# Five sets of down-projection weight sums moved behind the first product's loads, one of four subtractions on VectorE, the sums respread over the stages before

## The chip, the cores and the metric

The kernel runs on one core of one Trainium2 chip. Its time is the device time of one execution in microseconds (us); lower is better. Of the engines of a core, five matter here: TensorE (PE in the profile; PEld is its weight load), VectorE (DVE), ScalarE (ACT), GpSimd (POOL) and SyncE (SP), which in this kernel issues the DMAs.

## The reference

One layer of a decoder trunk for 1024 positions of width 1024, in float32: a token mixer (an RWKV-7 head group beside a causal convolution) and then a gated MLP with a short causal convolution. The change touches the MLP:

```python
def _conv_ffn(h, ffn_up, ffn_conv_w, ffn_conv_b, ffn_down):
    hid = h @ ffn_up.astype(h.dtype)
    hid = _causal_dwconv(hid, ffn_conv_w, ffn_conv_b)
    gate, up = hid[..., :D_FF], hid[..., D_FF:]
    return (jax.nn.gelu(gate, approximate=True) * up) @ ffn_down.astype(h.dtype)
```

Here D_FF is 2816: ffn_up is 1024 x 5632, ffn_down 2816 x 1024, and the convolution is 3 positions wide.

## The kernel before

**Products in three parts.** A float32 product is made from two halves of each operand. `split` (line 167) makes them: ScalarE casts the operand to the matmul type (the high part, `wh` or `w` for a weight, `a` for an activation), then an engine subtracts that from the operand (the low part, `wl`, or a second `w` or `a`). Three matmuls per tile follow: high by high, high by low, low by high (line 140). The subtraction for a weight runs on GpSimd, in `ffn_down` on VectorE (line 1140 sets that). `weight` loads a weight tile (line 175) and splits it; the last load issued is kept in `self.load`, the last low part in `self.low`.

**Seven products for eight.** The second half of the MLP's up-projection and the whole down-projection use sums of weight blocks and of activation blocks, so that seven block products give what eight would. A set of weight sums takes four 128x512 blocks b11, b12, b21, b22 and makes four results in place, with four operations on GpSimd (`four_sums`, line 1090).

**Who makes the sums.** For the up-projection, `act_sums` makes the activation sums `S` in twelve steps, and `shared` runs 16 blocks over them, each of 60 matmuls: five weights, 12 matmuls each. The first block loads its sums from DRAM; each of the other 15 loads four blocks of ffn_up (line 1056) into one of two groups of four buffers and calls `four_sums` itself, two blocks ahead of its use. For the down-projection, the generator `weight_sums` makes 12 sets (11 of ffn_down, and as third the one of the first shared block). Each set is four loads of 256 KB (line 1111), four GpSimd operations and four stores to DRAM (line 1114), from which products of `ffn_down` load their weights later. Its buffers hold two sets.

**The order of the stages.** The `gates` stage (a first pass over part of the up-projection); then six plain blocks (`PLAIN`, `ffn_pair`), each followed by `beside`, which takes one step of each generator handed to it and holds the step's instructions back behind a gate, a low part and a load of the block; then the 16 shared blocks; then `ffn_down` with seven products X, Y, ... of 11 steps j each (a step: split an activation, load and split a weight, 12 matmuls). The tile scheduler orders instructions on each engine by priority and expected readiness. `issue_after(x)` adds that an instruction is not placed ahead of x, on the same engine; SyncE's queue issues DMAs in order, and a DMA waits for the one eight earlier.

**Where the sets are made before.** Three sets in `gates`, one after each of the six plain blocks, and the last three in the first product, by `rest` on odd steps. There the call stands under high priority (`with first():`), and nothing holds its instructions: the scheduler put those three sets at the head of the shared stage, some 240 us ahead of the first product. In `shared` all four sums are GpSimd's.

Of the kernel before, what the change touches and what calls it, by code (L numbers as in the profile page):

```python
# [17 lines left out]
ALU = mybir.AluOpType  # L18
# [4 lines left out]
P = 128  # L23
# [79 lines left out]
class Trunk:  # L103
# [934 lines left out]
    def shared(self, i, S, A22, act0, act1, raws):  # L1038

        nc = self.nc  # L1040
        temp = lambda: self.f2p.tile([P, HALF], F32, tag="f2", name=self.nm("acc"))
        kview = lambda t: t.rearrange("p (k m) -> p k m", k=4)
        up = self.a["ffn_up"]

        def add(out, x, y):
            with self.tc.high_priority():
                nc.vector.tensor_tensor(out, x, y, ALU.add)

        if raws is None:
            T = lambda n: self.weight(kview(self.usums[n - 1]), [P, 4, P])  # L1050
            b22 = lambda: self.weight(up[FT + i, 1], [P, 4, P])
        else:
            with self.tc.high_priority():
                b11, b12, b21, b22r = raws
                for n in (1, 3, 0, 2):
                    self.load = nc.sync.dma_start(kview(raws[n]), up[n % 2 * FT + i, n // 2])
                t3 = self.wp.tile([P, HALF], F32, tag="wr", bufs=3, name=self.nm("t3"))
                self.four_sums(b11, b12, b21, b22r, t3)

            def pair(raw):  # L1060
                with self.tc.high_priority():
                    hi, lo = (self.wp.tile([P, HALF], F32R, tag=t, bufs=2, name=self.nm(t)) for t in ("wh", "wl"))
                    self.low = self.split(hi, lo, raw, True)[1]
                return kview(hi), kview(lo)

            T = lambda n: pair((b12, b11, t3, b21)[n - 1])
            b22 = lambda: pair(b22r)
        x, y, z = (self.bank() for _ in range(3))
        self.four(x, T(2), S[2], True, True)
        add(act1, act1, x)  # L1070
        self.four(y, T(1), S[1], True, True)
        W = temp()
        add(W, act1, y)
        self.four(z, T(3), S[3], True, True)
        add(x, W, z)
        self.four(y, b22(), S[4], False, True)
        add(y, act1, y)
        self.four(z, T(4), A22, False, True)
        add(z, act1, z)
        two = [temp() for _ in range(2)]  # L1080
        self.taps(0, i, 1, y, two[0])
        nc.vector.tensor_tensor(act0, act0, two[0], ALU.mult)
        self.taps(1, i, 0, z, act1)
        nc.scalar.activation(z, act1, AF.Gelu_apprx_tanh)
        self.taps(1, i, 1, x, two[1])
        nc.vector.tensor_tensor(act1, z, two[1], ALU.mult)

    def four_sums(self, b11, b12, b21, b22, t3):

        sub = lambda o, x, y, op=ALU.subtract: self.nc.gpsimd.tensor_tensor(o, x, y, op)  # L1090
        sub(t3, b22, b12)
        sub(b12, b12, b11)
        sub(b11, t3, b11, ALU.add)
        sub(b21, b21, b11)

# [41 lines left out]
    def ffn_down(self, acts, sums):  # L1137
        nc = self.nc
        first = self.tc.high_priority
        self.low_pool = False  # L1140
        A11, A12, A21, A22 = acts[0][:HT], acts[0][HT:], acts[1][:HT], acts[1][HT:]
        B = lambda r, c: lambda j: self.a["ffn_down"][c, ORDER[r * HT + j]]
        T = lambda n: lambda j: self.sums[n - 1, j]
        X = [self.bank() for _ in range(4)]
        Y = [self.bank(t) for t in ("pb", "pb", "pn", "pn2")]
        halves = lambda: [row[:, c * 512:(c + 1) * 512] for row in (self.row("nrow", 4) for _ in range(2)) for c in range(2)]
        four = lambda: [self.tp.tile([P, 512], F32, tag="tp", name=self.nm("c")) for _ in range(4)]

        def tt(out, a, b, op=ALU.add):
            nc.vector.tensor_tensor(out, a, b, op)  # L1150
            return out

        def s3(j):
            return tt(self.f2p.tile([P, HALF], F32, tag="f2", name=self.nm("s3")), A11[j], A21[j], ALU.subtract)

        def product(banks, src, wt, start, after, then=lambda j: None, held=(), soon=True):
            ops, n = [], HT - len(held)
            for j in range(HT):
                with first():
                    hi, lo = self.pair("a", self.h1p)  # L1160
                    self.split(hi, lo, src(j))
                    then(j)
                wh, wl = self.weight(wt(j), [P, 512], held=self.h1p if j % 2 else None) if j < n else held[j - n]
                op = (hi, wh), (hi, wl), (lo, wh)
                if j >= n:
                    ops.append(op)
                else:
                    for t in range(4):
                        mms(banks[t], t, op, start and j == 0, j == HT - 1)

            ins = []
            for t in range(4):
                for i, op in enumerate(ops):
                    ins += mms(banks[t], t, op, False, i == len(held) - 1)
                with first() if soon else ExitStack():
                    after(t)
            self.chain(ins)

        def mms(ps, t, op, start, stop):
            return [self.mm(ps, a[:, t * P:(t + 1) * P], w, start=start and i == 0, stop=stop and i == 2, skip=True)  # L1180
                    for i, (a, w) in enumerate(op)]

        def norm(h, t, c, f, src, junk):
            nc.scalar.activation(junk, src, AF.Square, accum_out=self.fss[:, 4 * h + t, c:c + 1])
            tt(f, src, self.post_ffn[:, c * 512:(c + 1) * 512], ALU.mult)

        def rest(j):
            if j % 2:
                next(sums, None)

        s1, s7 = halves(), halves()
        product(X, lambda j: A11[j], B(0, 0), True, lambda t: nc.scalar.copy(s1[t], X[t]), rest)
        list(sums)
        product(Y, s3, T(3), True, lambda t: nc.scalar.copy(s7[t], Y[t]))
        c11 = four()
        product(X, lambda j: A12[j], B(1, 0), False, lambda t: norm(
            0, t, 0, c11[t], X[t], self.f2p.tile([P, 512], F32, tag="f2", name=self.nm("junk"))))
        c21 = four()
        late = []

        def hold(j, every=2):

            if j % every == 1 and len(late) < HELD:
                home = self.hp if len(late) < HELD - 1 else self.ap
                late.append(self.weight(B(1, 1)(HT - HELD + len(late)), [P, 512], held=home))


        def after4(j):
            tt(A22[j], A21[j], A22[j])

        def after5(j):
            hold(j, 3)
            tt(A11[j], A22[j], A11[j], ALU.subtract)

        def after6(j):
            hold(j)
            tt(A12[j], A12[j], A11[j], ALU.subtract)

        product(Y, lambda j: A22[j], T(4), False, lambda t: tt(c21[t], s1[t], Y[t]), after4)
        product(X, lambda j: A22[j], T(1), True, lambda t: tt(s7[t], s7[t], X[t]), after5)  # L1220

        def second(t):
            tt(c21[t], c21[t], Y[t])
            tt(s1[t], s1[t], Y[t])
            norm(1, t, 0, c21[t], c21[t], Y[t])
            tt(s7[t], s7[t], s1[t])
            norm(1, t, 1, s7[t], s7[t], Y[t])
            self.ffn_out(4 + t, (c21[t], s7[t]), ready[4] if t == 3 else self.load_x1(4 + t, self.f2p, "f2"))

        def last(t):  # L1230
            tt(s1[t], s1[t], X[t])
            norm(0, t, 1, s1[t], s1[t], X[t])
            self.ffn_out(t, (c11[t], s1[t]), ready[t])

        with first():
            ready = [self.load_x1(t, self.ap, "act") for t in (0, 1, 2, 3, 7)]
        product(Y, lambda j: A11[j], T(2), True, second, after6, soon=False)
        product(X, lambda j: A12[j], B(1, 1), False, last, held=late)


    def run(self):
        nc = self.nc
# [5 lines left out]
        with ExitStack() as ctx:  # L1248
# [5 lines left out]
            sums = self.weight_sums()  # L1254
# [7 lines left out]
            ss = self.act_sums(h0, h1, S)  # L1262
            for i in range(PLAIN):
                nc.sync.dma_start(self.plain[i], self.ffn_pair(1, h1, i, temp))
                self.beside(sums, ss, ss)
            list(ss)
            raws = [self.h1p.tile([P, HALF], F32, tag="h", name=self.nm("b")) for _ in range(8)]

# [246 lines left out]
```

## Time and profile before

| what | value |
|---|---|
| median of 3 runs | 1285.8 us (1285.29 to 1287.09) |
| the profiled execution, its own time | 1284.83 us |
| its span, first to last instruction | 1283.1 us |
| mean granted TensorE clock | 0.984 |
| shared blocks 1 and 2 | 820 to 865 us |
| shared blocks 3 to 16 | 865 to 1063 us |
| products 1 and 2 of `ffn_down` | 1063 to 1123 us |
| products 3 to 7 | 1123 to 1283 us |

The profile shows one execution. A row of a group of instructions has line, engine, operation, output and inputs by name, count, busy time, mean duration, and idle time of the engine ahead of them with what ended it. A row of the waits has the engine and what it was about to do, what it waited for, the us in total, the number of waits and the longest. A row of a timeline has start and duration in us, the operation, how many in a row (x4), and in brackets the idle time ahead with what ended it. A row of the windows has the stretch, its length, the busy time of PE, PEld, DVE, ACT and POOL (with counts), the granted TensorE clock, the busy share of the DMA engines and their GB/s. The plain, shared and down-projection stages are read apart, since different engines wait in them.

### The profile page before, as it was taken

How to read it: one execution, taken by the hardware profiler on the slowest of the kernel's cores; microseconds unless marked ns; L12 is line 12 of the kernel's file. 1: busy time of each engine (PE TensorE's matmuls, PEld its weight loads, DVE VectorE, ACT ScalarE, POOL GpSimd, SP SyncE). 2: the span in 40 equal slices, each digit the busy share in tenths (PEclk: the TensorE clock that was granted, in tenths of full speed). 3: DMA queues.
4: the chain of work that ended last, by engine and by line, in shares of the span. 5: the costliest groups of instructions: out<-in, count | busy, mean ns of one | idle time of the engine just before them, and what ended most of it. 6: DMA issues, size and time to landing. Idle time of an engine off the chain costs nothing.

```text
span 1283.1 us, 22908 instructions
## 1 busy us (share of the span) xinstructions
PE 1215.2 (95%) x8388; PEld 979.9 (76%) x8388; DVE 912.6 (71%) x1570; ACT 728.2 (57%) x1516; POOL 517.9 (40%) x456
## 2 busy tenths in 40 slices
PE   6989999999999989999999999869999999999997
PEld 4767777787778867787798787657887878888885
DVE  5286998997679989995711756736765778569668
ACT  6563563655844865666742778625555555554451
POOL 4343320011113332344452698798888860000001
PEclk9999998999999999999999999989999999999999
DMA  7644442343343451233364998963222216346423
GB/s 237 174 134 137 118 130 75 98 133 126 107 132 87 127 193 57 93 91 111 112 173 128 335 343 295 349 201 106 76 74 74 82 54 218 99 130 206 126 81 131
DMA packets 104992, 184.64 MB, mean 144 GB/s; under 512 B 15184, under 2 KB 21712, under 8 KB 104880
## 3 DMA queue, kind: packets, MB, share of 16 engines
q1 hardware_dynamic: 104880, 183.18, 45.1%
q8 instruction: 66, 1.08, 0.3%
q14 instruction: 46, 0.38, 0.1%
HBM read 139.49 MB, written 43.65 MB: 143 GB/s over the span
## 4 chain that ended last, share of the span: by engine, by line
PE 45%; DVE 11%; DMA 6%; POOL 5%; issue 3%; ACT 3%; SPq 0%; POOLq 0%; DVEq 0%; ACTq 0%
PE pb L140 20%; PE pe L140 11%; PE xs L140 9%; POOL wl L167 3%; DVE pc L423 2%; PE Y L140 2%; POOL b L1090 2%; PE pc L140 2%; DMA b<-ffn_up 1%; DMA sums<-b 1%; DMA act<-early 1%; DVE nrow L1150 1%; DVE x L1134 1%; DMA pt<-mixd 1%; DMA x1d<-nrow 1%
## 5 line engine op out<-in xcount | busy, mean ns | idle before, releaser
L167 POOL TENSOR_TENSOR wl<-wr,wh 128x512 fp32r<-128x512 f32 (+1 forms) x145 | 188.9, 1304 | 219.9 <-ACT wh L167 190.9
L140 PE MATMUL pb<-h,wh 128*128 128x512 f32 (+3 forms) x720 | 229.6, 398 | 3.1 <-ACT wh L167 1.6
L140 PE MATMUL pb<-f,wh 128*128 128x512 f32 x592 | 188.0, 398 | 3.9 <-DVE pt L907 1.7
L167 ACT CAST wh<-wr 128x512 fp32r<-128x512 f32 (+1 forms) x184 | 113.0, 615 | 130.0 <-issue 36.3
L423 DVE SCALAR_TENSOR_TENSOR pc<-c,params,pc 128x512 f32<-128x512 f32 x232 | 174.2, 751 | 8.2 <-ACT pc L420 4.1
L140 PEld LDWEIGHTS pb<-h,wh 128*128 128x128 f32 (+2 forms) x720 | 131.9, 189 | 35.9 <-ACT wh L167 3.7
L140 PE MATMUL pb<-h,wl 128*128 128x512 f32 (+3 forms) x360 | 146.6, 407 | 2.1 <-POOL wl L167 2.0
L140 PEld LDWEIGHTS pb<-f,wh 128*128 128x128 f32 x592 | 109.9, 189 | 28.9 <-ACT wh L167 3.8
L140 PE MATMUL pb<-f,wl 128*128 128x512 f32 x296 | 117.7, 398 | 2.4 <-POOL wl L167 2.4
L1090 POOL TENSOR_TENSOR b<-b,b 128x512 f32<-128x512 f32 x78 | 104.2, 1341 | 7.0 <-DMA sums<-b 3.5
L162 POOL TENSOR_TENSOR ss<-var,mhalf 128x1 f32<-128x1 f32 x16 | 11.0, 693 | 223.2 <-DVE ss L1131 198.6
L167 POOL TENSOR_TENSOR wl<-b,wh 128x512 fp32r<-128x512 f32 x60 | 77.9, 1299 | 31.5 <-ACT wh L167 29.4
L140 PEld LDWEIGHTS pb<-h,wl 128*128 128x128 f32 (+2 forms) x360 | 67.7, 188 | 20.5 <-POOL wl L167 4.3
L167 ACT CAST wh<-b 128x512 fp32r<-128x512 f32 x60 | 37.0, 618 | 81.6 <-PE pb L140 34.4
L140 PE MATMUL pe<-f,wh 128*128 128x512 f32 x256 | 79.7, 393 | 0.1
L140 PEld LDWEIGHTS pb<-f,wl 128*128 128x128 f32 x296 | 55.8, 189 | 16.9 <-POOL wl L167 4.6
L167 DVE TENSOR_TENSOR a<-act,a 128x512 fp32r<-128x512 f32 x66 | 44.6, 693 | 22.9 <-ACT a L167 20.6
L167 ACT CAST a<-act 128x512 fp32r<-128x512 f32 x66 | 39.5, 618 | 37.3 <-PE Y L140 20.5
L140 PEld LDWEIGHTS pe<-f,wh 128*128 128x128 f32 x256 | 48.1, 189 | 10.1 <-ACT wh L167 0.5
L140 PE MATMUL xs<-f,wh 128*128 128x512 f32 x176 | 54.5, 391 | 0.4 <-DVE act L987 0.4
L713 POOL TENSOR_TENSOR XG<-r,GE 64x256 f32<-64x256 f32 x30 | 20.8, 694 | 84.3 <-DVE r L732 79.3
L140 PE MATMUL pe<-f,wl 128*128 128x512 f32 x128 | 50.8, 397 | 3.8 <-POOL wl L167 3.8
(431 smaller groups left out, 2986.8 us busy)
## 6 DMA issues: line engine op xcount, KB each, us to landing
wr<-ffn_up SPq DMA_DIRECT2D x81, 256.0 KB, 2.8
wr<-w_in SPq DMA_DIRECT2D x80, 256.0 KB, 2.9
b<-ffn_up SPq DMA_DIRECT2D x64, 256.0 KB, 2.6
b<-ffn_down SPq DMA_DIRECT2D x44, 256.0 KB, 4.5
sums<-b SPq DMA_DIRECT2D x44, 256.0 KB, 3.9
wr<-sums SPq DMA_DIRECT2D x44, 256.0 KB, 2.7
lows<-wl SPq DMA_DIRECT2D x40, 256.0 KB, 3.3
wl<-lows SPq DMA_DIRECT2D x40, 256.0 KB, 2.7
```

Of the source, the lines that this page charges most:

```text
L140: return self.nc.tensor.matmul(out, lhsT, rhs, start=start, stop=stop, skip_group_check=skip)
L162: self.nc.gpsimd.tensor_tensor(out, v[:, :n], self.mhalf[:, :n], ALU.pow)
L167: return self.nc.scalar.copy(hi, src), eng.tensor_tensor(lo, src, hi.bitcast(F32), ALU.subtract)
L423: nc.vector.scalar_tensor_tensor(out, c[:, j:j + HALF], w(j), acc, ALU.mult, ALU.add)
L713: nc.gpsimd.tensor_tensor(x[64:128], R[64:128, gs], w.GE[64:128, c, gs].unsqueeze(2).broadcast_to([64, 4, CH]), ALU.mult)
L1090: sub = lambda o, x, y, op=ALU.subtract: self.nc.gpsimd.tensor_tensor(o, x, y, op)
L1134: nc.vector.scalar_tensor_tensor(x, f[c], s[:, 1:2], x, ALU.mult, ALU.add)
L1150: nc.vector.tensor_tensor(out, a, b, op)
```

## The change

Three edits.

- `four_sums` takes an engine for its second operation, b12 - b11. `shared` hands it VectorE: 15 operations. The sets of `weight_sums` keep GpSimd for all four.
- After the plain blocks, a step of `weight_sums` is taken at blocks 0, 1, 3 and 4 only (four sets, not six). `act_sums` takes three steps at each of the first two blocks and two at the others (before: two at each), so that its twelve steps are done after the fifth block, not the sixth.
- In the first product, `rest` is called after the weight's load, on even steps j, not under high priority, and its instructions are held behind that step's weight load (`self.load`) and low part (`self.low`). Five sets are left for it. The call `list(sums)` behind the first product goes.

```diff
-                self.four_sums(b11, b12, b21, b22r, t3)
+                self.four_sums(b11, b12, b21, b22r, t3, nc.vector)
...
-    def four_sums(self, b11, b12, b21, b22, t3):
+    def four_sums(self, b11, b12, b21, b22, t3, eng=None):
...
-        sub(b12, b12, b11)
+        (eng or self.nc.gpsimd).tensor_tensor(b12, b12, b11, ALU.subtract)
...
                     self.split(hi, lo, src(j))
+                    if then is not rest:
+                        then(j)
+                wh, wl = self.weight(wt(j), [P, 512], held=self.h1p if j % 2 else None) if j < n else held[j - n]
+                if then is rest:
                     then(j)
-                wh, wl = self.weight(wt(j), [P, 512], held=self.h1p if j % 2 else None) if j < n else held[j - n]
...
         def rest(j):
-            if j % 2:
-                next(sums, None)
+            if j % 2 == 0:
+                with self.tc.issue_after(self.load.ins), self.tc.issue_after(self.low.ins):
+                    next(sums, None)
...
-        list(sums)
...
-                self.beside(sums, ss, ss)
+                self.beside(*[sums] * (i % 3 < 2), *[ss] * (3 if i < 2 else 2))
```

Line numbers in the changed kernel: the moved subtraction is line 1092, the other sums stay on 1090; lines behind the middle of the file are 3 higher.

Three places in the engines' queues show it. First GpSimd at the head of the shared stage. `wl_` are low parts, `t_` and `b_93..`/`b_92..` sums of shared blocks 2 and 3, `b_11...` sums of the sets. Before:

```order
L167 TENSOR_TENSOR wl_9420<-wr_9417,wh_9419 128x512
L1090 TENSOR_TENSOR b_9320<-b_9320,b_9319 128x512
L1090 TENSOR_TENSOR b_11309<-b_11309,b_11307 128x512
L1090 TENSOR_TENSOR b_9316<-b_9316,b_9315 128x512
L1090 TENSOR_TENSOR b_11370<-b_11370,b_11368 128x512
L1090 TENSOR_TENSOR b_9319<-t_1486_9467,b_9319 128x512
L1090 TENSOR_TENSOR b_9315<-t_1505_9592,b_9315 128x512
L1090 TENSOR_TENSOR b_11368<-b_11368,b_11367 128x512
L1090 TENSOR_TENSOR b_9321<-b_9321,b_9319 128x512
L167 TENSOR_TENSOR wl_9476<-b_9319,wh_9475 128x512
```

After, at the same place:

```order
L167 TENSOR_TENSOR wl_9369<-wr_9366,wh_9368 128x512
L1090 TENSOR_TENSOR t_1478_9435<-b_9290,b_9288 128x512
L1090 TENSOR_TENSOR t_1497_9560<-b_9286,b_9284 128x512
L167 TENSOR_TENSOR wl_9388<-wr_9385,wh_9387 128x512
L1090 TENSOR_TENSOR b_9287<-t_1478_9435,b_9287 128x512
L1090 TENSOR_TENSOR b_9283<-t_1497_9560,b_9283 128x512
L1090 TENSOR_TENSOR b_9289<-b_9289,b_9287 128x512
L1090 TENSOR_TENSOR b_9285<-b_9285,b_9283 128x512
L167 TENSOR_TENSOR wl_9444<-b_9287,wh_9443 128x512
```

The operations of the three sets and the b12 - b11 of blocks 2 and 3 are gone from between the low parts of the first block (`wl_9420`, now `wl_9388`, is its last) and the first low part of the second (`wl_9476`, now `wl_9444`). The moved b12 - b11 stand on VectorE, `L1092`, behind the taps and the first additions of the stage:

```order
L907 SCALAR_TENSOR_TENSOR acc_9273<-pb_9236,params,acc_9273 128x510
L920 TENSOR_TENSOR acc_9229<-pb_9192,acc_9273 128x512
L1047 TENSOR_TENSOR xs_99<-acc_9345,pe_9307 128x512
L1092 TENSOR_TENSOR b_9288<-b_9288,b_9287 128x512
L1092 TENSOR_TENSOR b_9284<-b_9284,b_9283 128x512
L1047 TENSOR_TENSOR xs_100<-act_9292,xs_100 128x512
L907 SCALAR_TENSOR_TENSOR acc_9404<-xs_100,params,acc_9404 128x511
```

On GpSimd, the sum that writes `b_9287` overwrites what this subtraction of `b_9288` reads, so it comes after it.

Second, SyncE's queue at the first product. `wr_` are weights of the steps j, `act_` activations fetched back, `b_` loads of a set, `sums<-` its stores. Before, weights follow each other, and step 5's is `wr_11443`:

```order
L1288 DMA act_11246<-early 128x512
L175 DMA wr_11405<-ffn_down 128x512
L1288 DMA act_11254<-plain 128x512
L1288 DMA act_11247<-early 128x512
L1288 DMA act_11255<-plain 128x512
L175 DMA wr_11443<-ffn_down 128x512
L175 DMA wr_11465<-ffn_down 128x512
L175 DMA wr_11487<-ffn_down 128x512
```

After, step 5's is `wr_11411`:

```order
L1291 DMA act_11214<-early 128x512
L175 DMA wr_11373<-ffn_down 128x512
L1291 DMA act_11222<-plain 128x512
L1291 DMA act_11215<-early 128x512
L1291 DMA act_11223<-plain 128x512
L1111 DMA b_11321<-ffn_down 128x512
L1111 DMA b_11322<-ffn_down 128x512
L1111 DMA b_11379<-ffn_down 128x512
L1111 DMA b_11380<-ffn_down 128x512
L1111 DMA b_11381<-ffn_down 128x512
L1111 DMA b_11382<-ffn_down 128x512
L175 DMA wr_11411<-ffn_down 128x512
```

Six loads of the second and third of the five sets stand ahead of it; two more (`b_11319`, `b_11320`) stand ahead of the activations.

Third, GpSimd behind the last low part of the shared stage. Before, the small operations of the output norm follow (`ss_`), near the end of the kernel:

```order
L167 TENSOR_TENSOR wl_11169<-t_1712_11125,wh_11168 128x512
L167 TENSOR_TENSOR wl_11186<-b_9322,wh_11185 128x512
L167 TENSOR_TENSOR wl_11203<-b_9321,wh_11202 128x512
L162 TENSOR_TENSOR ss_12933<-var_12935,mhalf 128x1
L162 TENSOR_TENSOR ss_12953<-var_12955,mhalf 128x1
```

After, 16 operations of four sets stand there; the first set of the five stands among the low parts of the two last shared blocks:

```order
L167 TENSOR_TENSOR wl_11154<-b_9290,wh_11153 128x512
L167 TENSOR_TENSOR wl_11171<-b_9289,wh_11170 128x512
L1090 TENSOR_TENSOR b_11322<-b_11322,b_11320 128x512
L1092 TENSOR_TENSOR b_11320<-b_11320,b_11319 128x512
L1090 TENSOR_TENSOR b_11319<-b_11322,b_11319 128x512
L1090 TENSOR_TENSOR b_11382<-b_11382,b_11380 128x512
L1090 TENSOR_TENSOR b_11321<-b_11321,b_11319 128x512
```

So the GpSimd work that stood at the head of the shared stage stands at the head of the down-projection.

## The prediction

> **What bounds the kernel now.** The page first: TensorE is busy for nearly the whole span, at a clock near full, and the chain that ended last is mostly its own.
>
> ```profile
> span 1283.1 us, 22908 instructions
> PE 1215.2 (95%) x8388; PEld 979.9 (76%) x8388; DVE 912.6 (71%) x1570; ACT 728.2 (57%) x1516; POOL 517.9 (40%) x456
> PE 45%; DVE 11%; DMA 6%; POOL 5%; issue 3%; ACT 3%; SPq 0%; POOLq 0%; DVEq 0%; ACTq 0%
> ```
>
> So time can be had only where TensorE waits or is slowed. The windows by stage show where (columns: stretch, length, busy time of PE, PEld, DVE, ACT, POOL, granted clock, DMA share, GB/s); the fourth row is an undisturbed pair of shared blocks.
>
> ```profile
> 760.00:820.00 60.00, 56.93 (x244) 44.89 (x243) 42.71 (x65) 46.70 (x97) 51.70 (x42) 1.00 0.90 320
> 820.00:865.00 45.00, 31.71 (x112) 22.92 (x111) 18.42 (x27) 15.67 (x33) 40.45 (x33) 0.85 0.74 259
> 865.00:1063.00 198.00, 196.70 (x852) 157.56 (x851) 132.97 (x190) 110.84 (x232) 160.34 (x122) 1.00 0.28 84
> 1007.46:1035.09 27.63, 27.63 (x121) 22.07 (x120) 18.03 (x27) 15.13 (x32) 23.69 (x19) 1.00 0.29 86
> 1063.00:1123.00 60.00, 59.91 (x264) 49.24 (x263) 41.66 (x66) 32.21 (x63) 0.00 (x0) 1.00 0.46 145
> ```
>
> Shared blocks 1 and 2 take 45.0 us; a later pair takes 27.6. The loss is 17.4 us, at a clock of 0.85, while GpSimd is busy 40.45 of 45. In the other 14 shared blocks TensorE is busy 196.70 of 198, in products 1 and 2 59.91 of 60, with GpSimd idle. TensorE's waits between 820 and 866 give the causes:
>
> ```profile
> PE pe L140 <- ACT wh L167: 4.7, 1, 4.7
> PE pe L140 <- POOL wl L167: 4.2, 3, 2.2
> PE xs L140 <- DVE s L167: 3.1, 1, 3.1
> PE pb L140 <- DVE pe L1047: 0.9, 1, 0.9
> PE pb L140 <- DVE acc L1047: 0.4, 1, 0.4
> ```
>
> They sum to 13.3 us; the other 4.1 of the 17.4 are matmuls at a lower clock behind the gaps. The ScalarE wait is GpSimd's in disguise: that cast takes a finished sum as input. GpSimd's timeline there:
>
> ```profile
> 828.85 1.28 POOL L1090 TENSOR_TENSOR b<-b,b 128x512 f32<-128x512 f32 x1 [3.46 <-DMA sums<-b]
> ...
> 838.77 5.45 POOL L1090 TENSOR_TENSOR b<-b,b 128x512 f32<-128x512 f32 x4
> 844.19 2.49 POOL L1090 TENSOR_TENSOR b<-t,b 128x512 f32<-128x512 f32 x2
> 846.63 2.50 POOL L1090 TENSOR_TENSOR b<-b,b 128x512 f32<-128x512 f32 x2
> 849.09 2.50 POOL L167 TENSOR_TENSOR wl<-b,wh 128x512 fp32r<-128x512 f32 x2
> 851.54 5.00 POOL L1090 TENSOR_TENSOR b<-b,b 128x512 f32<-128x512 f32 x4
> ```
>
> GpSimd works without a gap at 1.25 us an operation, and the second block's first low part comes at 849.09. It also sat 3.46 us behind a store of a set, whose buffer a held-up sum needed.
>
> **Edit 1: three sets leave the head of the shared stage.** In the changed order six sum operations of the three sets go from between 828.85 and 849.09 (7.5 us at 1.25), and two b12 - b11 go to VectorE (2.5 us); the 3.46 us wait on a store has no cause left. That is up to 13.5 us of earliness for the second block's first low part. What is late next is still GpSimd: within block 1's 13.8 us (half of 27.63) it has to run four low parts, six sums and one low part of block 2, 11 x 1.25 = 13.8 us, behind a cast that itself waits for a sum. I estimate 3.3 us of wait there, 1.7 in block 1 for the low parts, and half a us elsewhere: 5.5 us left of 17.4, a **gain of 12**. Bounds: 9.2 (7.5 for the sums ahead, 1.7 for the wait that one of them causes in block 1) and 17.4. I lie between because the new count of GpSimd operations just equals the time there is.
>
> The low clock goes with the gaps. Two windows of 4 us show it:
>
> ```profile
> 844.00:848.00 4.00, 1.85 (x4) 1.16 (x4) 2.09 (x3) 1.79 (x4) 4.00 (x5) 0.64 0.70 238
> 848.00:852.00 4.00, 1.82 (x5) 1.31 (x5) 0.00 (x0) 0.00 (x0) 4.00 (x4) 0.50 0.65 201
> ```
>
> Behind the 4.7 us gap the clock is 0.50. The Trainium skill (TensorE: Matmul & The Clock Gate, Part 1: The HAM clock gate) says that the clock halves only after an idle window of about 3.4 us; by that rule the 3.3 us I leave would cost no clock and the gain would be up to 1 us more. Since this trace is at 0.50 after one longer gap, it does not decide that.
>
> **Edit 2: b12 - b11 of 15 shared blocks on VectorE.** 15 operations leave GpSimd, but GpSimd is not late in the later blocks: it waits there for buffers that TensorE frees. Rows of the waits from 866 to 1048, of GpSimd and of VectorE:
>
> ```profile
> POOL wl L167 <- ACT wh L167: 25.7, 27, 2.6
> DVE acc L907 <- ACT fcarry L900: 15.7, 10, 1.6
> DVE pb L1047 <- PE pb L140: 16.9, 8, 3.2
> ```
>
> VectorE's share of it, 15 x 0.69 = 10.4 us, or 15 x 1.8 = 27 us with contention, lies in its 65 us of idle time (198 - 132.97), such as these waits. A new wait comes with it: GpSimd's third sum overwrites b11, which the moved subtraction reads, so GpSimd's queue, with the low parts behind it, waits for VectorE's queue, which itself waits up to 3.2 us for TensorE. GpSimd has 37.7 us idle in 14 blocks (198 - 160.34), 2.7 a block, and gains 1.25 a block: 3.9 against 3.2. I take **0**; the bounds are 0 and the 10.4 us of VectorE work should nothing cover it.
>
> **Edit 3: sums respread over the plain blocks.** Two sets fewer on GpSimd, the same `act_sums` work a block earlier on VectorE and ScalarE, which have 17 and 13 us idle of 60. The last `s` parts were the 3.1 us wait above; that is in edit 1's 17.4. TensorE idles 3.07 us in 760 to 820. I take **0**, bounds 3.1 gained, and, with one third more `act_sums` work in the first two blocks, as much lost.
>
> **Edit 4: five sets in products 1 and 2.** Two costs. First the loads. Product 1's loads already arrive just in time:
>
> ```profile
> 1064.00:1066.00 2.00, 2.00 (x11) 1.65 (x10) 2.00 (x5) 2.00 (x6) 0.00 (x0) 1.00 1.04 402
> 1067.17 11.44 SPq L175 DMA_DIRECT2D wr<-ffn_down x6
> 1072.50 0.62 ACT L167 CAST w<-wr 128x512 fp32r<-128x512 f32 x1 [4.16 <-DMA wr<-ffn_down]
> 1077.22 1.52 PE L140 MATMUL xs<-w,a 128*128 128x512 f32 x6
> ```
>
> The DMA engines run at 402 GB/s; step 5's weight arrives at 1072.5, and TensorE uses it at 1077.22, 4.7 us later. The change issues six or eight loads of 256 KB ahead of it, 1.6 or 2.1 MB at 402 GB/s, 3.9 or 5.2 us. With a cast (0.62) and a subtraction on VectorE (0.68 to 1.8) behind it, the weight is ready between 1077.7 and 1080.1: 0.5 to 2.9 us late, I take **2**.
>
> Second, GpSimd's 16 sums there meet VectorE, which subtracts the low parts in this stage. What such a meeting costs is seen in the shared stage:
>
> ```profile
> 996.41 1.29 POOL L1090 TENSOR_TENSOR b<-b,b 128x512 f32<-128x512 f32 x1
> 997.66 1.74 POOL L167 TENSOR_TENSOR wl<-t,wh 128x512 fp32r<-128x512 f32 x1
> ...
> 996.49 1.76 DVE L1082 TENSOR_TENSOR act<-act,acc 128x512 f32<-128x512 f32 x1
> ...
> L1082 DVE TENSOR_TENSOR act<-act,acc x16: 677/890/1816, 842.3 to 1071.5; 128x512 f32<-128x512 f32 x16
> ...
> 1060.00:1080.00 20.00, 19.91 (x88) 16.10 (x87) 19.62 (x33) 13.46 (x28) 0.35 (x1) 1.00 0.76 267
> 1080.00:1100.00 20.00, 20.00 (x90) 16.57 (x89) 13.40 (x22) 10.96 (x20) 0.00 (x0) 1.00 0.41 117
> ...
> L167 DVE TENSOR_TENSOR a<-act,a 128x512 fp32r<-128x512 f32 x12 | 8.2, 684 | 2.8 <-ACT a L167 2.8
> ```
>
> The addition starts with GpSimd's operation and ends when that one and its own 0.6 us are through: 1.76 us; alone it takes 0.68. A step of product 1 takes 2.73 us (60 us for 22 steps) and holds two such subtractions; next to a steady GpSimd these take 3.5 us, 0.8 too long. Sixteen sums at 1.75 us last 28 us, eight steps: 6.4 us if VectorE has no lead. Over both products VectorE's 41.66 us and 16 x 1.25 = 20 us of GpSimd are 61.7 of 60: 1.7 us if the slack spreads evenly. I take **4**, between the two. Both costs together are 6; bounds 0 and 20.
>
> The Trainium skill (SBUF — State Buffer, Who interferes with whom) has GpSimd and a VectorE operation with two SBUF inputs exclude each other for a whole instruction; by it all 16 sums could lock VectorE, 20 us by the rows, which is the second rival below.
>
> **The sum.** 1284.83 - 12 + 6 + 0 + 0 = 1278.8 for an execution like the profiled one. The median of the runs is 1.0 us above it, so **1280 us**; 0.2% (2.6 us) is about what a measurement of this kernel can tell from no change.
>
> **The rivals.**
>
> *The products cover the sets.* The weights of steps 6 and on are loaded early enough, VectorE has a lead, nothing is late: the gain stays whole, 1285.8 - 12 = 1274, at most 1268.4. For it: VectorE is at 13.40 of 20 after 1080, and TensorE is busy 59.91 of 60 now. Against it: 19.62 of 20 before. 0.2.
>
> *The sets starve the products (slower).* GpSimd's 16 sums and VectorE take turns from 1075 on, VectorE falls behind, each sum's 1.25 us is TensorE's: 20 lost against 12 gained, 1294. It is slower from 12 us lost on, three quarters of the sums. For it: the 19.62. Against it: the 60 us of the two products hold nearly all the work. 0.16.
>
> *The head stays as it was.* If the raw loads and the six sums in series still end last, each low part in block 2 waits as now, only about 5 us are gained, and edit 4 takes them: 1286. Whether the sets could leave no mark because the scheduler brings them forward again is answered by the order: only the first of the five stands in the shared stage. 0.14.
>
> **How the numbers follow.** The forecast has 0.50, the rivals 0.20, 0.16 and 0.14. The forecast and the first rival are faster: 0.70; the third is the same, 0.14; the second is slower, 0.16. The range goes from 1268, the whole head loss won with the products covered, to 1292, most of the second rival: 8 in 10 and the unknown of edit 4.
>
> **What would show it.** TensorE's waits in the first two shared blocks fall from 13.3 to about 5.5 us, the stretch from 45.0 to about 33, the clock there above 0.85. In the other shared blocks TensorE stays within 1.3 us of the stretch, with the moved subtractions at 0.7 to 1.8 us each. In products 1 and 2, which take 60 now, about 66; VectorE's subtractions have a mean over 1 us while GpSimd runs, and TensorE has waits for `w` and `a` of line 167 that it has not now, among them one for step 5's weight behind a DMA. I am wrong if the two first blocks still take over 36 us, or if the two products take under 62 or over 72.

## The result, and the profile after

The changed kernel takes 1289.12 us (median of 20 runs), the kernel before 1285.37 us (20 runs): a ratio of 1.0031, with a 95% interval of 1.0017 to 1.0045. It is slower by about 4 us, where 6 us faster was forecast; 1289.12 lies inside the range of 1268 to 1292, on the wrong side of its middle. The profiled execution took 1289.33 us, with a span of 1287.6.

First the chain that ended last, on the page of the changed kernel: GpSimd's share has grown from 5% to 12%, TensorE's has fallen from 45% to 36%.

```profile
PE 36%; POOL 12%; DVE 11%; issue 6%; DMA 5%; ACT 3%; SPq 0%; POOLq 0%; DVEq 0%; ACTq 0%
```

The stages are now cut at the first matmul of each, so that they hold equal work. Windows of the kernel before: shared blocks 1 and 2, shared blocks 3 to 16, products 1 and 2.

```profile
820.12:867.37 47.25, 33.96 (x121) 24.79 (x120) 19.12 (x28) 17.63 (x36) 42.35 (x35) 0.86 0.72 252
867.37:1063.20 195.83, 194.53 (x842) 155.77 (x840) 132.47 (x189) 109.09 (x232) 158.32 (x120) 1.00 0.28 84
1063.20:1123.46 60.26, 60.17 (x266) 49.45 (x264) 41.46 (x66) 32.47 (x62) 0.00 (x0) 1.00 0.46 144
```

The same of the changed kernel, with products 3 to 7 as fourth row:

```profile
821.26:855.75 34.49, 30.08 (x122) 23.12 (x121) 22.89 (x33) 16.88 (x37) 22.61 (x19) 0.95 0.38 133
855.75:1059.42 203.67, 194.92 (x841) 156.57 (x840) 155.75 (x201) 108.56 (x230) 148.40 (x111) 1.00 0.32 92
1059.42:1127.96 68.54, 63.28 (x266) 50.16 (x264) 54.13 (x66) 32.12 (x61) 25.35 (x16) 0.98 0.72 246
1127.96:1287.60 159.64, 150.01 (x661) 123.69 (x659) 120.16 (x207) 68.71 (x136) 6.28 (x8) 0.98 0.41 135
```

The first two blocks gained 12.8 us (47.25 to 34.49). Blocks 3 to 16 lost 7.8, products 1 and 2 lost 8.3, and the rest takes 159.64 us in both (1283.1 - 1123.46 before). The shared stage began 1.1 us later (820.12 against 821.26); of the stages ahead of it the change touches only the plain blocks, which the prediction put at 0, and among the runs below that start scatters from 818 to 823. -12.8 + 7.8 + 8.3 + 1.1 is 4.4, the 4.5 us between the spans.

TensorE's waits in the changed kernel, one fence each for blocks 1 and 2, blocks 3 to 16, and products 1 and 2:

```profile
PE pe L140 <- POOL wl L167: 2.7, 2, 2.1
PE pe L140 <- ACT wh L167: 1.4, 2, 0.8
PE pb L140 <- ACT wh L167: 0.3, 1, 0.3
```

```profile
PE pb L140 <- POOL wl L167: 4.4, 7, 1.3
PE xs L140 <- POOL wl L167: 4.3, 7, 1.0
```

```profile
PE pb L140 <- DVE wl L167: 3.8, 1, 3.8
PE xs L140 <- ACT w L167: 0.8, 1, 0.8
PE xs L140 <- DVE wl L167: 0.4, 1, 0.4
PE xs L140 <- DVE w L167: 0.3, 1, 0.3
```

At the head 4.4 us of waits are left of 13.3. In blocks 3 to 16, TensorE now waits once in each of the 14 blocks for a low part of GpSimd, 8.7 us in all. Before, in the same blocks, it waited three times, 1.2 us:

```profile
PE pb L140 <- POOL wl L167: 0.8, 1, 0.8
PE pe L140 <- POOL wl L167: 0.2, 1, 0.2
PE xs L140 <- POOL wl L167: 0.2, 1, 0.2
```

In the products it waits 5.3 us, most of it once, for VectorE. That is not the whole of their 8.3 us. The wait of 3.8 us ends at 1102.61, and behind it the granted clock is low:

```profile
1104.00:1106.00 2.00, 2.00 (x6) 1.59 (x5) 2.00 (x5) 0.77 (x2) 0.00 (x0) 0.50 0.28 103
1106.00:1108.00 2.00, 2.00 (x7) 1.55 (x6) 1.86 (x4) 0.97 (x3) 0.00 (x0) 0.69 1.01 380
```

At 0.50 and 0.69 these four us lose about 1.6 (an estimate from the two rows). The rest, some 1.4 us, was not taken apart.

Which low part is late is read from GpSimd's timeline around the start of a block. A shared block uses its five weights in the order T(2), T(1), T(3), b22, T(4): T(2), T(1) and T(4) are the sums made in place in b11, b12 and b21, T(3) is the sum t, and b22 is the raw block. Each needs its own low part. Before:

```profile
1006.53 1.30 POOL L167 TENSOR_TENSOR wl<-b,wh 128x512 fp32r<-128x512 f32 x1
1007.79 1.29 POOL L1090 TENSOR_TENSOR b<-t,b 128x512 f32<-128x512 f32 x1
1009.04 1.30 POOL L167 TENSOR_TENSOR wl<-b,wh 128x512 fp32r<-128x512 f32 x1
1010.28 1.83 POOL L1090 TENSOR_TENSOR b<-b,b 128x512 f32<-128x512 f32 x1
```

After, and TensorE's row that waits:

```profile
912.44 1.29 POOL L167 TENSOR_TENSOR wl<-b,wh 128x512 fp32r<-128x512 f32 x1
914.36 1.30 POOL L1090 TENSOR_TENSOR b<-t,b 128x512 f32<-128x512 f32 x1 [0.63 <-DVE b L1092]
915.74 1.29 POOL L1090 TENSOR_TENSOR b<-b,b 128x512 f32<-128x512 f32 x1
916.98 1.28 POOL L167 TENSOR_TENSOR wl<-b,wh 128x512 fp32r<-128x512 f32 x1
...
918.32 0.50 PE L140 MATMUL xs<-s,wl 128*128 128x512 f32 x1 [0.59 <-POOL wl L167]
```

Between the block's first low part (T(2)) and its second (T(1)) stood one sum of the next block, b11. Now two stand there, b11 and b21, and ahead of them GpSimd waits 0.63 us for the moved subtraction. The second low part starts 4.54 us behind the first (916.98 - 912.44), before 2.51. TensorE spends 2.72 us on the 12 matmuls of a weight, and the first low part was ready 1.1 us before TensorE took it (at 913.73, its first matmul at 914.85). So a distance of about 3.8 us costs nothing, and at 4.54 TensorE waits.

### The profile page after: what moved, and what is told of

The parts are those of the page before. It is cut to its first block, busy times and chain, and to the rows that moved or that the text cites. A ratio compares the mean times of both kernels' runs of the same rounds, so it can differ in the third digit from the quotient of the medians.

```text
span 1287.6 us, 22910 instructions
## 1 busy us (share of the span) xinstructions
PE 1218.3 (95%) x8388; PEld 982.8 (76%) x8388; DVE 950.1 (74%) x1585; ACT 727.4 (56%) x1516; POOL 506.2 (39%) x441
## 4 chain that ended last, share of the span: by engine, by line
PE 36%; POOL 12%; DVE 11%; issue 6%; DMA 5%; ACT 3%; SPq 0%; POOLq 0%; DVEq 0%; ACTq 0%
PE pb L140 17%; PE pe L140 8%; PE xs L140 7%; POOL wl L167 7%; POOL b L1090 3%; DMA b<-ffn_up 2%; PE Y L140 2%; DVE pc L423 2%; PE pc L140 2%; ACT wh L167 1%; DVE a L167 1%; DVE nrow L1150 1%; DVE x L1134 1%; POOL t L1090 1%; DMA act<-early 1%
## 5 line engine op out<-in xcount | busy, mean ns | idle before, releaser
L1090 POOL TENSOR_TENSOR b<-b,b 128x512 f32<-128x512 f32 x51 | 69.5, 1366 | 25.5 <-DMA b<-ffn_down 23.3
L167 DVE TENSOR_TENSOR a<-act,a 128x512 fp32r<-128x512 f32 x66 | 49.6, 771 | 23.2 <-ACT a L167 20.6
```

The source lines that it names most:

```text
L167: return self.nc.scalar.copy(hi, src), eng.tensor_tensor(lo, src, hi.bitcast(F32), ALU.subtract)
```

## The experiments

Each row's times come from the run's own profile, cut at the same first matmuls; the ratio stands against the kernel before on the same chip, with its 95% interval. "Pair" is blocks 1 and 2. Before, these are 47.25, 195.83 and 60.26; in the change 34.49, 203.67 and 68.54. A stage's time is that of one execution. The six kernels that keep the change's order in the shared blocks (the change, c, d, e, g, k) scatter from 202.6 to 204.3 us in blocks 3 to 16, and the five without sets in the products (before, c, e, h, j) from 59.9 to 60.3 there.

| run | pair 1 | blocks 3-16 | products 1, 2 | median | ratio |
|---|---|---|---|---|---|
| a_pool_b12 | 34.98 | 196.29 | 67.08 | 1282.56 | 0.9985 (0.9971 to 1.0000) |
| b_late_b21 | 30.76 | 193.09 | 65.83 | 1270.18 | 0.9884 (0.9862 to 0.9906) |
| c_no_sets | 34.79 | 202.66 | 60.05 | 1280.57 | 0.9957 (0.9939 to 0.9976) |
| d_no_sums | 34.74 | 202.63 | 60.85 | 1278.81 | 0.9951 (0.9933 to 0.9969) |
| e_dve_only | 44.56 | 203.05 | 60.02 | 1288.89 | 1.0026 (1.0015 to 1.0037) |
| g_free_stores | 35.78 | 203.23 | 72.3 | 1292.57 | 1.0051 (1.0034 to 1.0067) |
| i_late_b21_pool | 31.66 | 198.46 | 65.78 | 1277.67 | 0.9944 (0.9924 to 0.9963) |
| j_spread | 30.78 | 194.32 | 59.94 | 1266.56 | 0.9850 (0.9833 to 0.9866) |
| h_late_b21_in_shared | 31.04 | 210.00 | 59.94 | 1283.11 | 0.9979 (0.9961 to 0.9997) |
| k_old_spread | 34.55 | 204.33 | 63.27 | 1283.14 | 0.9993 (0.9971 to 1.0015) |

**a_pool_b12: the subtraction back on GpSimd.**

```diff
-                self.four_sums(b11, b12, b21, b22r, t3, nc.vector)
+                self.four_sums(b11, b12, b21, b22r, t3)
```

> The change with its VectorE subtraction taken back (all four sums of the shared blocks on GpSimd again). Theory: the 7.8 us that shared blocks 3 to 16 lost (195.8 to 203.7 from the first matmul of block 3 to that of product 1) come from the moved subtraction, so that stretch goes back to 196, the first two blocks stay near 34.5, the products near 68.5, and the time is about 1281. Rival: the blocks lost to the held-back set that now stands in the last ones, or to the loads there; then the stretch stays near 203 and the time near 1289.

Measured: blocks 3 to 16 take 196.29 us, 7.4 less than in the change. Their loss hangs on the moved subtraction, not on the held-back set or its loads. The profiled execution, 1278.06 us, is among the fastest of the ten; the median is 1282.56. The first pair takes 34.98, so of the 12.8 us gained there all but 0.5 come without the moved subtraction.

**e_dve_only: the kernel before with the moved subtraction alone.** The edit is the diff's first two pieces.

> The kernel before with only the second operation of the shared blocks' sums moved to VectorE. Theory: GpSimd's queue then again has b11 and b21 of the next block ahead of T(1)'s low part, so blocks 3 to 16 take 202 to 204 us where they took 195.8; the first two blocks may gain up to 3 us; products stay at 60.3; the time is 4 to 8 us above before. Rival: the loss needs the other edits; then 196 and no slower than before.

Measured: blocks 3 to 16 take 203.05 us, the loss of the change; the first pair gains 2.7. The median is 3.75 us above before (1285.14 on that chip), a little under the 4 expected. So the subtraction needs no other edit to do its harm.

**b_late_b21: the subtraction on VectorE, the fourth sum behind T(1)'s low part.**

```diff
+        if raws is not None:
+            with self.tc.high_priority(), self.tc.issue_after(self.low.ins):
+                nc.gpsimd.tensor_tensor(b21, b21, b11, ALU.subtract)
         W = temp()
```

(`four_sums` leaves its fourth operation out for the shared blocks.)

> The change with the fourth sum (b21) of a shared block held behind that block's own low part of T(1), the subtraction still on VectorE. Theory (order): what costs is that GpSimd's b11 and b21 of the next block stand back to back ahead of the low part of T(1); with b21 behind it, blocks 3 to 16 take 195 to 198 us and the time is about 1282. Rival (handoff): GpSimd's 0.63 us wait for VectorE in each block is the cost; then 200 or more. Rival (VectorE too full): 203.7 as in the change, time 1289.

Measured: 193.09 us, less than before the change and less than expected, and 1270.18 us; the first pair, too, takes 3.7 us less than in the change (30.76). From block 5 to block 14 a pair of blocks takes 27.20 us in each case, 120 matmuls at 0.227. GpSimd's timeline of this run:

```profile
901.87 1.30 POOL L167 TENSOR_TENSOR wl<-b,wh 128x512 fp32r<-128x512 f32 x1
903.79 1.29 POOL L1093 TENSOR_TENSOR b<-t,b 128x512 f32<-128x512 f32 x1 [0.62 <-DVE b L1095]
905.04 1.30 POOL L167 TENSOR_TENSOR wl<-b,wh 128x512 fp32r<-128x512 f32 x1
906.30 1.29 POOL L1074 TENSOR_TENSOR b<-b,b 128x512 f32<-128x512 f32 x1
```

The second low part is 3.17 us behind the first, under the 3.8 worked out above, and TensorE no longer waits for it; 0.62 of it are still GpSimd's wait for VectorE. The rows of that wait and of the subtraction, from 866 to 1030 us, of the change and then of this run:

```profile
POOL b L1090 <- DVE b L1092: 6.9, 11, 0.6
...
L1092 DVE TENSOR_TENSOR b<-b,b 128x512 f32<-128x512 f32 x12 | 21.1, 1756 | 0.4 <-POOL t L1090 0.4
```

```profile
POOL b L1093 <- DVE b L1095: 6.9, 11, 0.6
...
L1095 DVE TENSOR_TENSOR b<-b,b 128x512 f32<-128x512 f32 x11 | 19.3, 1754 | 0.1
```

Handoff and contention are the same in both, 6.9 us and 1.75 us a subtraction; only the place of b21 differs, and the 7.8 us are gone. So neither the handoff nor VectorE's load costs TensorE anything by itself in these blocks: the pairs from block 5 to 14 run without a wait.

**i_late_b21_pool: b21 held back, and all four sums on GpSimd.** The edit is shown against b_late_b21.

```diff
-                self.four_sums(b11, b12, b21, b22r, t3, nc.vector, False)
+                self.four_sums(b11, b12, b21, b22r, t3, None, False)
```

> The change with b21 behind T(1)'s low part (as in b_late_b21) and all four sums on GpSimd. Theory: GpSimd's order is then that of before, b12 and b11 ahead of T(1)'s low part, so blocks 3 to 16 take 195 to 196.5 us, 2 to 3 more than with b12 on VectorE (193.1); that difference is what edit 2 gains when the order is kept. Rival: the order of b21 alone made b_late_b21 fast; then 193 here too.

Measured: 198.46 us, over the 195 to 196.5 expected. Its middle pairs take 27.65 to 27.90 us as before; the surplus lies in the first (29.67) and the last (29.95). Against b_late_b21 it is 5.4 us, 2.8 of them in the five middle pairs: with the order kept, VectorE's subtraction is a gain.

**c_no_sets and d_no_sums: what the sets cost in the products.** In the first the five sets are left out (products read older sums), in the second only their sums (raw blocks are stored).

```diff
         def rest(j):
-            if j % 2 == 0:
-                with self.tc.issue_after(self.load.ins), self.tc.issue_after(self.low.ins):
-                    next(sums, None)
+            return
```

```diff
-            self.four_sums(*b, b[3])
+            if self.low_pool:
+                self.four_sums(*b, b[3])
```

> The change without the five held-back sets: their loads, sums and stores are left out, and products read the sums of step 5 in place of those of steps 6 to 10. Theory: all of the 8.3 us that products 1 and 2 lost are these sets': the two take 60.3 again, and the time is about 1281. Rival: part comes from elsewhere, such as the later weights' order; then more than 62.

> The change with the loads and stores of the five held-back sets kept and only their sums on GpSimd left out, so that the raw blocks are stored. Theory (VectorE and GpSimd take turns): the products' loss is mostly VectorE's subtractions at 1.75 instead of 0.68 us; without them the two products take about 62, the time is about 1283. Rival (DMA): the loads and stores themselves are late; then 66 to 68, and the time stays at 1287 to 1289.

Measured: 60.05 us without the sets, as expected, and 60.85 with their loads and stores but no sums, less than the 62 expected. So the loads and stores of the sets cost 0.8 us, and GpSimd's sums 7.7 of the 8.5, in whatever way they do. VectorE's low parts from 1070 to 1106 us in the change, and over as long a window from the same point of the stage (1067 to 1103) without the sums:

```profile
L167 DVE TENSOR_TENSOR a<-act,a 128x512 fp32r<-128x512 f32 x5 | 6.6, 1338 | 0.0
L167 DVE TENSOR_TENSOR w<-wr,w 128x512 fp32r<-128x512 f32 x5 | 6.4, 1285 | 3.9 <-ACT w L167 3.9
```

```profile
L167 DVE TENSOR_TENSOR a<-act,a 128x512 fp32r<-128x512 f32 x5 | 3.3, 685 | 0.0
L167 DVE TENSOR_TENSOR w<-wr,w 128x512 fp32r<-128x512 f32 x8 | 5.5, 689 | 8.4 <-ACT w L167 8.4
```

In the window with GpSimd's sums these subtractions have a mean of 1.3 us, without them 0.69. (VectorE's three other groups in the first window have means of 0.99 to 1.12.)

**g_free_stores: the sums made, but the stores not waiting for them** (they take a tile that is long ready).

```diff
-                nc.sync.dma_start(dst(n), b[t])
+                nc.sync.dma_start(dst(n), b[t] if self.low_pool else self.ready)
```

> The change, in which the stores of the five held-back sets take an activation tile that is long ready, in place of the sums, so that SyncE's queue does not wait for GpSimd; the sums are still made on GpSimd, and products read wrong sums. Theory (VectorE and GpSimd take turns): products 1 and 2 still take 65 to 68 us, VectorE's subtractions there still reach 1.7 us. Rival (queue): what costs is that loads of weights stand behind stores that wait for sums; then 61 to 63.

Measured: 72.3 us (1057.67 to 1130.00), longer than the change's 68.5. Freeing the stores does not win the time back, but the run does not settle the rival either: the stores and the loads now reach the DMA queue in one burst, and TensorE waits 4.4 us for casts of weights where it waited 0.8. In the change, from 1056 to 1112 us, SyncE's queue stood 9.2 us at stores that waited for GpSimd's sums, with weights behind them. How the 7.7 us divide between VectorE's longer subtractions and weights that came later stays open.

**k_old_spread: the change with the old spread after the plain blocks**, which leaves three sets for the first product.

```diff
-                self.beside(*[sums] * (i % 3 < 2), *[ss] * (3 if i < 2 else 2))
+                self.beside(sums, ss, ss)
```

> The change with the old spread after the plain blocks (a set after each of the six, two steps of the activation sums at each), so that three sets are left for the first product. Theory: TensorE waits 2 to 3 us for the last s of the activation sums in the first shared block again, so the first two blocks take 36 to 38 us where the change has 34.5; products 1 and 2, with three sets and not five, take 63 to 66; blocks 3 to 16 stay near 203; the time is 1286 to 1289. Rival: the respread gains nothing at the head; then 34 to 35 there, and the time 1284 to 1286.

Measured: TensorE's wait for the last `s` is back,

```profile
PE xs L140 <- DVE s L167: 2.8, 1, 2.8
```

but the first pair takes 34.55 us, as in the change: the waits for GpSimd and for casts there are 1.5 us and not 4.4. That GpSimd gets ahead while TensorE waits for `s` is a reading of this, not tested. The products take 63.27, 5.3 less than with five sets. The respread brought nothing at the head and cost what two more sets cost in the products.

**h_late_b21_in_shared and j_spread: the five sets in the shared stage.** Both are b_late_b21 with `rest` empty. In h a whole set is taken behind every second block; in j one operation behind T(3)'s low part and one behind b22's, over blocks 3 to 13 (the generator then yields ahead of each operation).

```diff
+                if m in (2, 4, 6, 8, 10):
+                    self.beside(sums)
```

```diff
+    def step(self, m):
+        if 2 <= m < 13:
+            with self.tc.issue_after(self.low.ins), self.tc.issue_after(self.load.ins):
+                next(self.sets, None)
...
         add(x, W, z)
+        self.step(m)
         self.four(y, b22(), S[4], False, True)
         add(y, act1, y)
+        self.step(m)
```

> b_late_b21 with the five held-back sets' sums moved from the first product into shared blocks 3 to 13, one operation behind the low part of T(3) and one behind that of b22, their loads a step earlier. Theory: GpSimd has gaps of 1.4 us there while it waits for buffers, so blocks 3 to 16 take 193 to 197 us, products 1 and 2 60.3, and the time is 1262 to 1267. Rival: ten operations a block at 1.25 us, with VectorE taking turns, leave too little of 13.6 us; then 200 or more, and 1270 or more.

> b_late_b21 with the five held-back sets in shared blocks 3 to 11, one whole set behind every second block, so that in GpSimd's queue a sum of the set stands beside the next block's b11 ahead of T(1)'s low part. Theory (order): each of the five pairs of blocks loses about 1 to 3 us on TensorE's waits for GpSimd, blocks 3 to 16 take 198 to 206 us, products 60.3, the time is 3 to 10 us above that of j_spread with the same amount of work. Rival (only the amount of GpSimd work counts): 194 to 195 as in j_spread, no difference.

Windows of blocks 3 to 16, of h and then of j:

```profile
851.53:1061.53 210.00, 197.65 (x842) 155.70 (x840) 151.40 (x202) 110.59 (x230) 169.68 (x128) 1.00 0.39 123
```

```profile
848.98:1043.30 194.32, 194.15 (x841) 156.16 (x840) 152.77 (x202) 110.00 (x230) 167.81 (x128) 1.00 0.42 133
```

GpSimd has the same 128 operations in both, 169.68 and 167.81 us. Where the sums stand, and with them when their loads and stores are issued, makes 15.7 us, more than expected. In h the five pairs with a set take 31.1 us each, the two others 27.2. TensorE's waits there, from 851 to 990 us, are of several kinds:

```profile
PE pb L140 <- ACT wh L167: 3.6, 8, 0.5
PE pb L140 <- DVE acc L1047: 3.5, 4, 0.9
PE pb L140 <- POOL wl L167: 1.4, 4, 0.4
PE pe L140 <- POOL wl L167: 1.4, 4, 0.4
```

Some are VectorE's: a set's sum ahead of the next block's t makes the moved subtraction, and VectorE's queue behind it, late. That reading was not tested; in j, in the same stretch, VectorE waits 5.3 us for t, in h 4.6, and TensorE waits only 0.2. j takes 1266.56 us and beats both kernels, 1.5% under before, with products at 59.94.

## Why the prediction was wrong, step by step

**The step that failed** is edit 2, which it put as "I take **0**; the bounds are 0 and the 10.4 us of VectorE work should nothing cover it". It measured 7.8 us lost, shown from both sides: 7.4 back when it is undone, 7.2 lost when it is made alone. The bound held, its reason did not. The prediction named the new wait, GpSimd behind VectorE's queue, and covered it with idle time per block, 3.9 us against 3.2. The wait was only 0.63 us. But an average of idle time says nothing of one low part that TensorE needs 2.7 us behind another: what stood ahead of that one grew by the wait and by one more sum. So the prediction's own sign for these blocks, TensorE within 1.3 us of the stretch, failed: it was 8.75 us off (203.67 - 194.92). GpSimd's idle time was elsewhere in the block, in front of T(4)'s and b22's low parts. In the trace of the changed kernel b21 runs ahead of T(1)'s low part in each of blocks 3 to 15, but the prediction had read the order of GpSimd's queue only at the head and at the end of the stage. That b21 alone is enough to take away is shown by b_late_b21; what b21 would cost without the 0.63 us was not tried.

**Edit 1 had the mechanism right, and its size with some luck.** 12 us were forecast, 12.8 measured. The stretch read, 820 to 865, ended 2.4 us ahead of block 3, so the loss was 19.6 us (47.25 - 27.63) and not 17.4, and 6.9 stayed and not 5.5: two misses that partly cancel. GpSimd was late next, as forecast: block 2 waits 3.2 us where 3.3 were forecast, 2.10 of them for its low part, and block 1 waits 1.2 where 1.7 were.

**Edit 3** was taken as 0 at the head, and k_old_spread agrees (34.55 against 34.49). That it would send two more sets into the products was counted in edit 4. (Three steps of `act_sums` for two are one half more work in the first two blocks, not the third that the bound was reasoned with.)

**Edit 4** had the size within its bounds, 6 forecast and 8.3 measured, and VectorE's subtractions longer beside GpSimd, as forecast. Its split was wrong: of the two terms, the late loads (2) measured 0.8 with the stores; the sums, put at 4 by the turns of GpSimd and VectorE, measured 7.7, in which the turns are not parted from stores that wait for sums. Step 5's weight was late behind a DMA, as forecast, but by 0.8 us. The lower clock behind a long wait was in neither term. The largest wait, 3.8 us, came in the second product, where a low part stood behind two other operations on VectorE, all three taking 1.6 to 1.8 us while GpSimd made sums. VectorE had also been idle 3.1 us in the few us before, for casts of weights that came late. VectorE's timeline there:

```profile
1097.44 1.78 DVE L167 TENSOR_TENSOR a<-s,a 128x512 fp32r<-128x512 f32 x1
1099.25 1.63 DVE L1150 TENSOR_TENSOR s<-act,act 128x512 f32<-128x512 f32 x1
1100.81 1.75 DVE L167 TENSOR_TENSOR wl<-wr,wh 128x512 fp32r<-128x512 f32 x1
```

**The rivals.** The one that ended slower, products starved by 20 us, was not the case, and neither were the other two: the products did lose, and the head did gain. The sign came from a stage in which no rival had been priced. (The 12 us from which the starved products would be slower are three fifths of its 20, not three quarters.) With edit 2 at its measured 7.8, the forecast's own sum is 1284.83 - 12 + 6 + 7.8 = 1286.6, near no change.

**The clock.** The 3.2 us left in block 2 did cost clock: they are a wait of 2.10 us that ends at 841.58, with two of 0.77 and 0.33 just before it, and the granted clock is 0.50 in the next window. The Trainium skill (TensorE: Matmul & The Clock Gate, Part 1: The HAM clock gate), weighed in the prediction, gives an idle window of about 3.4 us; this trace speaks for a shorter one. But in b_late_b21 a wait of 2.20 us that ends at 1083.82, with none close before it, left the clock at 1.00 from 1080 to 1088. So these runs give no single length of a wait from which the clock falls.

```profile
840.00:842.00 2.00, 0.42 (x1) 0.42 (x2) 1.97 (x4) 0.62 (x3) 2.00 (x2) 0.75 0.35 131
842.00:844.00 2.00, 2.00 (x6) 1.52 (x6) 0.50 (x1) 0.60 (x1) 0.76 (x1) 0.50 0.46 136
```

## What to carry to other kernels

Idle time of an engine covers new work only if it lies ahead of the instruction that someone waits for: take the place in the queue and the gap between two of its results, not an average per block. Where an operation leaves an in-order engine, see what moves up into its place; here it was one that nobody needed yet. The same 20 operations of five sets, put where the engine waits for a buffer anyway, cost the shared blocks 1.2 us (193.09 to 194.32), no more than executions scatter, and a whole set at a time 16.9 (to 210.00).

## What the runs showed of the hardware

When a VectorE subtraction and a GpSimd operation met, the one that started later paid. In 13 of the 15 blocks the moved subtraction started 0.08 us behind a low part of GpSimd and took 1.75 us, where 0.68 is its time alone; the low part kept its 1.29. Where VectorE had started first (an addition at 917.43), the GpSimd low part that began behind it at 918.22 took 1.76 us. And the loads and stores of the sets beside two products cost 0.8 us in d_no_sums, where no sum stood behind them; the DMA engines were busy 77% of that time, at 279 GB/s.
